# One hybrid layer (short convolution and RWKV-7): VectorE's order in phase 1 taken from a gap-filling clock, and general buffers handed out by the kernel

## The chip, the cores and the metric

The kernel runs on one core of one Trainium2 chip. The metric is device microseconds of one launch; 3 runs of the kernel before took 3189.91, 3191.65 and 3194.61 us, median 3191.65. The profile is one more execution of the same program.

## The reference

The input is 2048 rows of a new sequence and 8 x 4 rows of running ones, 1024 wide, all float32. What is computed, cut to its core:

```python
h = rmsnorm(x, norm_g)
p = h @ w_in                       # 4 x 1024 conv, 4 x 1024 + 128 rwkv, 2 x 1024 gate columns
u = cg * xin;  y_c = bg * conv3(u) * silu(zc)          # short convolution branch
xm = p_rwkv + (prev - p_rwkv) * mu_shift               # token shift, then r, k, v, wd, ad, zr
def step(S, inp):                                      # RWKV-7, 16 heads of 64, one step a token
    sa = einsum(S, -kk_t)
    S = S * d_t + sa * (kk_t * a_t) + v_t * k_t
    return S, einsum(S, r_t)
y_r = (groupnorm(ys) * ln_w + ln_b + bonus) * silu(zr)
m = sigmoid(gc) * (y_c @ w_out_c) + sigmoid(gr) * (y_r @ w_out_r)
y = rmsnorm(x + m @ w_o, final_g)
```

New convolution, shift and RWKV states are returned as well.

## The kernel before

**Tiling.** The sequence is cut into 4 sets of 512 tokens (NT); the last set carries the 32 running rows. Activations stand transposed, 128 channels by 512 tokens. Every float32 product is made of three fp32r matmuls of a high and a low part (XH, XL; whl holds both parts of a block of weights), so one block of 128 output channels is 8 x 3 matmuls of 512 columns into one bank `ip` (proj, L266). Weights are split into the two parts in the first set (ScalarE's cast, VectorE's subtraction, L225 and L249), stored, and loaded again ready split in later sets.

**Phase 1** (to about 2650 us) goes through the sets; in each through 8 pairs of heads, 32 pairs of set and heads in all. The main stream is the projection blocks (xin, cg, zc, bg and the two gates for the convolution, k, r, v, z for the next pair), whose results VectorE and ScalarE take out of the bank. Beside it run side tasks, Python generators (class Side, L309): keys (decays and scaled keys of the next pair), solve (a triangular inversion by 31 steps of two short VectorE operations, tt and X, behind a transpose Mi<-Mc, L930), merge, load, chain, out. The chain (rwkv_chain, L1091) is the recurrence: 8 steps a pair, each one TensorE `pa` = S x AR, VectorE `us` (two operations), TensorE `pb` = Xbd x us, the copy to `SV` (VectorE one half, then ScalarE the other, L1067), TensorE `pb` = BKt x SV, VectorE `S` (two operations). Near the end of phase 1 the first output products (oc) join the main stream. **Phase 3** is the rest of the output products and the final norm.

**What sets the order.** The program is traced by Python. A class Clock (L42) keeps a time for each engine and for each written box of a tile; every traced instruction is booked at the end of its engine's booked work or when its inputs are there, whichever is later (add, L91), with costs in ns from cost (L130). Side.run (L325) is called after each main matmul. It goes on with a side task only when the share of main work done asks for it, when the results it asked for are ready by the clock, and, for tasks that are not urgent, when VectorE's booked work reaches less than BACKLOG = 1800 ns past TensorE's. So the clock decides at which place among the main matmuls a side task's matmuls stand. After the trace the framework's compile-time scheduler puts the instructions of each engine in order, by trace order and by its own timing: one that it holds for not ready lets a later one go ahead. The order is then fixed; on the chip each engine takes its own list in turn and waits on semaphores.

The general buffers are the pool `tmp` (L403), eight buffers of 576 float32 a partition; the framework's scheduler gives out whichever is free.

Of the kernel before, what the change touches and what calls it, by code (L numbers as in the profile page):

```python
# [16 lines left out]
P = 128  # L17
# [23 lines left out]

class Clock:  # L42
# [3 lines left out]
    def __init__(self):  # L46
        self.t = dict.fromkeys(("PE", "DVE", "ACT", "POOL", "SP"), 0.0)
        self.log, self.home = {}, {}
        self.mode = (128, 128)
        self.held = {"DVE": [], "POOL": []}  # L50
# [25 lines left out]

    def name(self, ap):
        return self.home.get(ap.tensor.name, ap.tensor.name)
# [8 lines left out]

    def ready(self, aps):
        return max([e[4] for ap in aps for e in self._hits(ap)], default=0.0)

    def add(self, eng, outs, ins, cost, lag=60.0):  # L91
        start = max([self.t[eng]] + [e[4] for ap in ins for e in self._hits(ap) if e[6] != eng] +
                    [e[5] for ap in outs for e in self._hits(ap)])
        if eng == "POOL" or eng == "DVE" and sum(ap.space != PSUM for ap in ins) > 1:
            for s, e in self.held["POOL" if eng == "DVE" else "DVE"]:
                if s < start + cost and start < e:
                    start = e
            self.held[eng] = self.held[eng][-60:] + [(start, start + cost)]
        end = start + cost
        self.t[eng] = end  # L100
# [3 lines left out]
        for ap in outs:  # L104
            for p0, p1, f0, f1 in self.boxes(ap):
                old = self.log.setdefault(self.name(ap), [])
                old[:] = [e for e in old if not (p0 <= e[0] and e[1] <= p1 and f0 <= e[2] and e[3] <= f1)][-95:]
                old.append([p0, p1, f0, f1, end + lag, end, eng])


class Traced:
# [5 lines left out]
    def __getattr__(self, op):  # L117
        f = getattr(self.eng, op)

        def call(*a, **k):  # L120
# [5 lines left out]
            self.clock.add(self.name, outs, ins, self.cost(op, outs[0], ins, k), 200.0 if self.name == "PE" else 60.0)  # L126
# [3 lines left out]
    def cost(self, op, out, ins, k):  # L130
        n = out.free_size()
        if self.name == "PE":
            if op == "transpose":
                return 109.0
            lhs, rhs = k["lhsT"], k["rhs"]
            if rhs.dtype == F32R:
                mode, t = (P, P), 8 + 0.45 * n
            else:
                part = [next(x for x in (32, 64, 128) if v <= x) for v in (lhs.ap[0][1], lhs.free_size())]
                mode, t = tuple(part), 2 * max(0.84 * max(lhs.free_size(), n), 26.0) / (1 if part == [P, P] else 1.9)  # L140
            t += 170 * (mode != self.clock.mode)
            self.clock.mode = mode
            return t
        if self.name == "DVE":
            per = {"transpose": 1.6, "tensor_tensor_scan": 2.1}.get(op, 1.05)
            if op == "tensor_reduce":
                n = ins[0].free_size()
            return 150 + per * n
        if self.name == "ACT":
            return 200 + 0.84 * n + 90 * max(0, len(ins) - 1)  # L150
# [5 lines left out]
class Queue:  # L156
# [5 lines left out]
    def store(self, out, in_):  # L162

        self.due.append((out, in_))
        self.flush(2)

    def flush(self, most):
        while self.due and (len(self.due) > most or self.clock.ready([self.due[0][1]]) < self.clock.t["PE"]):
            self.dma_start(*self.due.pop(0))
# [10 lines left out]
def hybrid_kernel(tc, x_prompt, x_sample, state_conv, state_shift, state_rwkv, norm_g, w_in, conv_w,  # L180
# [26 lines left out]
    wraw_p = ctx.enter_context(tc.tile_pool(name="wraw", bufs=4))  # L207
    whl_p = ctx.enter_context(tc.tile_pool(name="whl", bufs=4))
    dram = ctx.enter_context(tc.tile_pool(name="dram", bufs=1, space=DRAM))
    ps_ip = ctx.enter_context(tc.tile_pool(name="ps_ip", bufs=3, space=PSUM))  # L210
# [98 lines left out]
    class Side:  # L309
# [15 lines left out]
        def run(self, upto, force=False):  # L325
# [3 lines left out]
            while self.given < goal and self.f0 <= upto and (force or max(self.due, pt_free(self.banks)) <= clock.t["PE"] and (  # L329
                    self.kind in URGENT or clock.t["DVE"] < clock.t["PE"] + BACKLOG)):  # L330
# [68 lines left out]
    nwt = ctx.enter_context(tc.tile_pool(name="nwt", bufs=1))  # L399
    con = ph1.enter_context(tc.tile_pool(name="con", bufs=1))  # L400
    xp = ph1.enter_context(tc.tile_pool(name="xp", bufs=1))
    rw = ph1.enter_context(tc.tile_pool(name="rw", bufs=1))
    tmp = ph1.enter_context(tc.tile_pool(name="tmp", bufs=8))  # L403
    ep = ph1.enter_context(tc.tile_pool(name="ep", bufs=2))
    sm = ph1.enter_context(tc.tile_pool(name="sm", bufs=2))
    ps_t = ph1.enter_context(tc.tile_pool(name="ps_t", bufs=2, space=PSUM))
    ps_a = ph1.enter_context(tc.tile_pool(name="ps_a", bufs=2, space=PSUM))
    ps_b = ph1.enter_context(tc.tile_pool(name="ps_b", bufs=1, space=PSUM))
# [22 lines left out]
    def stat_tile(i, xt, m):  # L431
        junk = tmp.tile([P, TW], F32, name="tmp").bitcast(BF16)[:, 0:D]
        A.activation(out=junk[0:m], in_=xt[0:m], func=AF.Square, accum_out=rstd[0:m, i:i + 1])

# [53 lines left out]
    V.transpose(X0.rearrange("p a b -> p (a b)"), xo0.rearrange("p a b c -> p (a b c)"))  # L488

# [61 lines left out]
    def to_cols(q, xt, cl, eng):  # L551
# [7 lines left out]
        split(XH[:, q * KG:(q + 1) * KG, cl:cl + P], XL[:, q * KG:(q + 1) * KG, cl:cl + P], xf, eng)  # L559

# [67 lines left out]
    def mixed_block(th, key, src, mb, alloc, end=None):  # L628
# [24 lines left out]
        def fin():  # L653
            if th < LAST:
                G.tensor_copy(carry[:, mb:mb + 1], o["q"][:, NT:NT + 1])
            if end:
# [18 lines left out]
    def conv_blocks(th, b):  # L675
# [25 lines left out]
        def cg_end():  # L701
            u = o["u"]
            cv = o["cv"] = ep.tile([P, NT + NSAMP], F32, name="cv", bufs=1)
# [24 lines left out]
        def zc_end():  # L728
            G.tensor_tensor(out=o["cv"][:, 0:nt], in0=o["cv"][:, 0:nt], in1=o["tz"][:, 0:nt], op=ALU.mult)

# [8 lines left out]
        def gate(nm, base, dst):  # L739
# [10 lines left out]
            def end():  # L750
                SP.dma_start(out=dst[th][b], in_=g["t"][:, 0:nt])
            return Block((nm, th, b), wcol(base, b), evac, begin, end)
# [22 lines left out]
    def rkvz_blocks(th, p):  # L775
# [14 lines left out]
        def z_end(zT):  # L790
# [3 lines left out]
            V.scalar_tensor_tensor(out=sz[:, 0:nt], in0=sz[:, 0:nt], scalar=1.0, in1=zT[:, 0:nt], op0=ALU.add, op1=ALU.mult)  # L794
            cur[(th, p)] = (got["r"], got["k"], got["v"], sz)
# [12 lines left out]
    def rwkv_keys(th, p, o):  # L808
# [20 lines left out]
        if samp:  # L829
# [3 lines left out]
            V.reciprocal(ss[0:NSAMP, 2 * TPS:], ss[0:NSAMP, 2 * TPS:])  # L833
        yield W["norm"], [up], 2
# [17 lines left out]
        if samp:  # L852
            V.tensor_tensor_scan(out=Gs[:, n:nt], data0=rst_s, data1=L[:, n:nt], initial=0.0, op0=ALU.mult, op1=ALU.add)
        yield W["scan"], [Gs[:, 0:nt]]
# [12 lines left out]
        A.activation(out=Pi[:, 0:nt], in_=Gs[:, 0:nt], func=AF.Exp, scale=DECAY)  # L867
# [755 lines left out]
```

## Time and profile before

| | |
|---|---|
| median of 3 runs | 3191.65 us |
| the profiled execution | 3193.32 us, span 3191.6 us |
| granted TensorE clock over the span | 0.992 |
| PE busy | 3092.0 us (97%), 21530 matmuls |
| PEld busy | 2596.5 us (81%) |
| DVE busy | 1992.5 us (62%), 5704 instructions |
| ACT busy | 1241.9 us (39%) |
| POOL busy | 309.6 us (10%) |
| chain that ended last | PE 69%, DVE 18%, ACT 5%, issue 5%, DMA 3% |

PE is TensorE's matmuls, PEld its weight loads, DVE is VectorE, ACT ScalarE, POOL GpSimd. All compute instructions come through one helper (L121) and all DMAs of SyncE through another (L172), so rows are told apart by tile names and not by lines: `ip` is a bank of a projection, `pt` a general PSUM bank, `pa`, `pb`, `us`, `SV` and `S` are the chain's. "x2" behind a float32 matmul is its two passes. A matmul's end is modelled, so matmuls that follow each other overlap in the rows.

### The profile page before, as it was taken

How to read it: one execution, taken by the hardware profiler on the slowest of the kernel's cores; microseconds unless marked ns; L12 is line 12 of the kernel's file. 1: busy time of each engine (PE TensorE's matmuls, PEld its weight loads, DVE VectorE, ACT ScalarE, POOL GpSimd, SP SyncE). 2: the span in 40 equal slices, each digit the busy share in tenths (PEclk: the TensorE clock that was granted, in tenths of full speed). 3: DMA queues.
4: the chain of work that ended last, by engine and by line, in shares of the span. 5: the costliest groups of instructions: out<-in, count | busy, mean ns of one | idle time of the engine just before them, and what ended most of it. 6: DMA issues, size and time to landing. Idle time of an engine off the chain costs nothing.

```text
span 3191.6 us, 55625 instructions
## 1 busy us (share of the span) xinstructions
PE 3092.0 (97%) x21530; PEld 2596.5 (81%) x21530; DVE 1992.5 (62%) x5704; ACT 1241.9 (39%) x2571; POOL 309.6 (10%) x517
## 2 busy tenths in 40 slices
PE   7999999999999999999999999999999999999998
PEld 6777777887777778877777789989889889778896
DVE  5687777776666666666666676766677664443332
ACT  5454445444333434434443334344444432211201
POOL 2011111111000001100101010000000000000000
PEclk9999999999999999999999999999999999999999
DMA  8786666644444444444444444434443469988863
GB/s 267 258 267 220 213 212 220 207 173 148 146 162 160 155 159 159 169 157 153 159 153 158 159 147 142 138 127 139 144 143 135 138 223 318 363 337 304 316 241 120
DMA packets 241504, 615.09 MB, mean 193 GB/s; under 512 B 33931, under 2 KB 143620, under 8 KB 187479
## 3 DMA queue, kind: packets, MB, share of 16 engines
q1 hardware_dynamic: 241094, 611.00, 55.8%
q8 instruction: 170, 2.79, 0.4%
q14 instruction: 96, 0.78, 0.1%
q0 software_dynamic: 144, 0.52, 0.0%
HBM read 452.10 MB, written 159.36 MB: 192 GB/s over the span
## 4 chain that ended last, share of the span: by engine, by line
PE 69%; DVE 18%; ACT 5%; issue 5%; DMA 3%; POOL 1%; SPq 0%; ACTq 0%; DVEq 0%; POOLq 0%
PE ip L121 49%; PE pt L121 10%; PE po L121 6%; PE pb L121 3%; DVE X L121 2%; DVE tmp L121 2%; DVE tt L121 2%; ACT tmp L121 2%; DVE Mi L121 2%; DVE whl L121 1%; DVE us L121 1%; PE pa L121 1%; DVE S L121 1%; DMA wraw<-in_w_in_dram 1%; ACT Xbd L121 1%
## 5 line engine op out<-in xcount | busy, mean ns | idle before, releaser
L121 PE MATMUL ip<-XH,whl 128*128 128x512 f32 (+3 forms) x7776 | 2105.1, 351 | 6.6 <-DVE gt L121 3.9
L121 PEld LDWEIGHTS ip<-XH,whl 128*128 128x128 f32 x7776 | 1342.0, 190 | 178.3 <-issue 27.5
L121 PE MATMUL ip<-XL,whl 128*128 128x512 f32 (+3 forms) x3888 | 1364.0, 351 | 2.7 <-POOL XL L121 2.6
L121 PEld LDWEIGHTS ip<-XL,whl 128*128 128x128 f32 x3888 | 738.5, 190 | 79.0 <-issue 7.0
L121 DVE TENSOR_TENSOR X<-X,tt 128x60 f32<-128x60 f32 (+24 forms) x992 | 211.7, 213 | 27.5
L121 DVE TENSOR_TENSOR tt<-Mi,X 128x60 f32<-128x60 f32 (+24 forms) x992 | 209.9, 212 | 27.4
L121 DVE SCALAR_TENSOR_TENSOR S<-pb,pe,sp 64x64 f32<-64x64 f32 x512 | 143.8, 281 | 106.6 <-PE pb L121 100.5
L121 ACT ACTIVATE sp<-S,pe 128x128 f32<-128x128 f32 x256 | 99.5, 400 | 244.7 <-DVE S L121 241.2
L121 ACT ACTIVATE tmp<-ip,vec 128x512 f32<-128x512 f32 (+2 forms) x174 | 103.2, 593 | 231.6 <-PE ip L121 230.2
L121 ACT COPY SV<-pb 64x64 f32<-64x64 f32 x256 | 53.3, 208 | 329.2 <-DVE SV L121 325.5
L121 DVE TENSOR_TENSOR whl<-wraw,whl 128x1024 fp32r<-128x1024 f32 x105 | 134.2, 1279 | 58.0 <-ACT whl L121 57.7
L121 PE MATMUL po<-whl,MH 128*128 128x512 f32 x544 | 170.4, 394 | 0.0
L121 DVE TENSOR_TENSOR us<-pa,P 64x64 f32<-64x64 f32 x512 | 110.2, 215 | 45.2 <-PE pa L121 33.7
L121 PEld LDWEIGHTS pb<-us,Xbd 128*128 128x128 f32 x512 | 85.9, 189 | 56.9 <-PE ip L121 21.5
L121 PE MATMUL ip<-RH,whl 128*128 128x512 f32 (+2 forms) x512 | 128.4, 341 | 1.7 <-DMA whl<-w_or 1.6
L121 PEld LDWEIGHTS pb<-SV,BKt 128*128 128x128 f32 x512 | 85.1, 189 | 54.6 <-ACT SV L121 45.9
L121 ACT CAST whl<-wraw 128x1024 fp32r<-128x1024 f32 x105 | 109.5, 1044 | 50.5 <-DMA wraw<-in_w_out_r_dram 14.8
L121 PE MATMUL pb<-SV,BKt 128*128 128x128 f32 x512 | 107.3, 291 | 17.4 <-ACT SV L121 17.3
L121 DVE TENSOR_TENSOR GM<-pt,mask_p 128x512 f32<-128x512 f32 x128 | 82.4, 685 | 64.4 <-PE pt L121 64.4
L121 PEld LDWEIGHTS po<-whl,MH 128*128 128x128 f32 x544 | 102.2, 188 | 24.0 <-DVE whl L121 0.3
L121 PE MATMUL pb<-us,Xbd 128*128 128x64 f32 x512 | 90.1, 258 | 23.7 <-DVE us L121 23.1
L121 ACT COPY Xbd<-Xo 32x256 f32<-32x256 f32 x128 | 88.1, 688 | 64.0 <-DVE Xo L121 61.9
(494 smaller groups left out, 3838.6 us busy)
## 6 DMA issues: line engine op xcount, KB each, us to landing
wraw<-in_w_in_dram SPq DMA_DIRECT2D x81, 512.0 KB
whl<-w_k SPq DMA_DIRECT2D x24, 1024.0 KB
whl<-w_r SPq DMA_DIRECT2D x24, 1024.0 KB
whl<-w_v SPq DMA_DIRECT2D x24, 1024.0 KB
whl<-w_z SPq DMA_DIRECT2D x24, 1024.0 KB
whl<-w_xin SPq DMA_DIRECT2D x24, 1024.0 KB
whl<-w_cg SPq DMA_DIRECT2D x24, 1024.0 KB
whl<-w_zc SPq DMA_DIRECT2D x24, 1024.0 KB
```

The source lines that it names most:

```text
L121: r = f(*a, **k)
```

## The change

Four things, all at trace time. (1) Clock.add books an operation of VectorE, ScalarE or GpSimd into the first gap among the last 200 booked ones that it fits in, from 3000 ns before TensorE's time on, never ahead of an operation of the same engine on the same tensor. TensorE's and SyncE's bookings are appended as before. (2) In phase 1 each VectorE instruction is noted with its begin time; behind phase 1 the list is sorted by it, and each instruction gets an edge to the one in front of it that orders the two and has no wait. (3) The costs are others, for TensorE by tiling and with a delay to the reader of its own. (4) The buffers `tmp` become eight buffers with fixed names; a class Ring gives out the one whose last use ends first by the clock, and the program frees each by a call. Tiles of other pools get names by which the clock knows which buffer they share. The instructions themselves, the loops, the weights of the side tasks and their spans are not changed.

```diff
     def add(self, eng, outs, ins, cost, lag=60.0):
-        start = max([self.t[eng]] + [e[4] for ap in ins for e in self._hits(ap) if e[6] != eng] +
+        start = max([self.t["PE"] - PAST if eng in self.busy else self.t[eng]] + [e[4] for ap in ins for e in self._hits(ap) if e[6] != eng] +
+                    [e[5] for ap in (*ins, *outs) for e in self._hits(ap) if e[6] == eng] +
+                    [self.touched.get((eng, ap.tensor.name), 0.0) for ap in (*ins, *outs)] +
                     [e[5] for ap in outs for e in self._hits(ap)])
+        if eng in self.busy:
+            start = self.gap(eng, start, cost)
...
+    def gap(self, eng, start, cost):
+        b = self.busy[eng]
+        if len(b) >= 200:
+            start = max(start, b[0][1])
+        i = len(b)
+        while i and b[i - 1][1] > start:
+            i -= 1
+        for s, e in b[i:]:
+            if s >= start + cost:
+                break
+            start = max(start, e)
+        return start
...
+class Ring:
...
+            home = min(self.open, key=self.ends)
+            self.open.remove(home)
+            t = self.pool.tile(self.shape, dtype, name="tmp", tag=home)
...
     def cost(self, op, out, ins, k):
...
-                mode, t = (P, P), 8 + 0.45 * n
+                mode, t, late = (P, P), 8 + 0.4375 * n, 175 + 0.43 * n
+            elif mode == (P, P):
+                t, late = max(1.667 * n + 3, 216.0), max(382.0 if n >= P else 328.0, 175 + 1.7 * n)
...
+            if mode != self.clock.mode:
+                t, late = t + 165, late + 225
+                self.clock.mode = mode
+            return t, late - t + SLACK
         if self.name == "DVE":
-            per = {"transpose": 1.6, "tensor_tensor_scan": 2.1}.get(op, 1.05)
+            per = {"transpose": 1.12 if n <= 256 else 1.86, "tensor_tensor_scan": 2.1, "reciprocal": 6.1}.get(op, 1.05)
...
-            return 150 + per * n
+            one = op == "scalar_tensor_tensor" and isinstance(k["scalar"], bass.AP)
+            return 145 + per * n + 58 * one
...
-                    self.kind in URGENT or clock.t["DVE"] < clock.t["PE"] + BACKLOG)):
+                    self.kind in URGENT or clock.load("DVE") < BACKLOG)):
...
-    tmp = ph1.enter_context(tc.tile_pool(name="tmp", bufs=8))
+    tmp = Ring(ph1.enter_context(tc.tile_pool(name="tmp", bufs=1)), [P, NT + 64], 8, clock)
...
     finish_sides()
+    clock.planning = False
+    for ops in clock.begun.values():
+        ops.sort(key=lambda o: o[0])
+        for (_, a), (_, b) in zip(ops, ops[1:]):
+            tc.add_manual_dep(b, a.name, mybir.DependencyInfo(
+                mybir.DependencyClass.NoSync, mybir.DependencyReason.DATA), reason="keep_in_program_order")
```

A matmul's result is ready for a reader on another engine 60 + (late - t + SLACK) ns after its booked end, with SLACK = 60; before it was 200 ns for each. A VectorE or GpSimd operation that reads two tiles of SBUF is kept off the intervals in which the other one of the two engines is booked with such an operation, in both kernels.

## Rows read from the trace of the kernel before

**Rows 1.** Stretches: us, busy us and count by engine, clock, DMA share, GB/s.

```profile
0.00:50.00 50.00, 30.10 (x195) 27.93 (x196) 28.44 (x67) 23.18 (x35) 18.51 (x55) 0.93 0.77 251
50.00:850.00 800.00, 771.09 (x5017) 611.10 (x5017) 569.79 (x1530) 386.42 (x727) 97.73 (x147) 0.99 0.65 213
850.00:1850.00 1000.00, 986.01 (x6536) 781.72 (x6533) 643.78 (x1944) 403.79 (x847) 102.51 (x189) 1.00 0.46 157
1850.00:2650.00 800.00, 782.06 (x6944) 724.78 (x6943) 546.12 (x1763) 329.58 (x781) 72.04 (x105) 0.99 0.45 151
2650.00:3192.00 542.00, 522.71 (x2847) 450.96 (x2845) 204.34 (x401) 98.96 (x182) 18.80 (x21) 0.99 0.78 284
```

**Rows 2.** TensorE's waits: who for whom, us in total, times, longest us.

```profile
PE pb L121 <- DVE us L121: 23.1, 39, 1.6
PE pb L121 <- ACT SV L121: 17.3, 29, 1.4
...
PE pt L121 <- DVE T L121: 3.5, 5, 1.0
PE pt L121 <- ACT Wm L121: 3.4, 7, 1.1
...
PE pa L121 <- DVE S L121: 1.9, 3, 0.9
```

**Rows 3.** Timeline from 258 us: start, us, engine, operation, [idle before <-releaser].

```profile
257.80 0.49 PE L121 MATMUL pa<-S,AR 128*128 128x128 f32 x2
...
258.35 2.05 DVE L121 STREAM_TRANSPOSE Mi<-Mc 128x1024 f32<-128x1024 f32 x1 [0.61 <-ACT Mc L121]
...
259.28 0.40 PE L121 MATMUL ip<-XL,whl 128*128 128x512 f32 x1
...
259.51 0.39 PE L121 MATMUL ip<-XH,whl 128*128 128x512 f32 x1
260.43 0.45 DVE L121 TENSOR_TENSOR us<-pa,P 64x64 f32<-64x64 f32 x2
...
261.02 0.41 PE L121 MATMUL pb<-us,Xbd 128*128 128x64 f32 x2 [1.12 <-DVE us L121]
```

**Rows 4.** Weight loads by form: count, busy us, mean ns, idle us before them, releasers.

```profile
L121 PEld LDWEIGHTS ip<-XH,whl 128*128 128x128 f32 x7776 | 1342.0, 190 | 178.3 <-issue 27.5 <-DVE gt L121 4.1 <-DVE whl L121 2.3
...
L121 PEld LDWEIGHTS pa<-S,AR 128*128 128x128 f32 x512 | 89.3, 190 | 24.8 <-DVE S L121 11.4
...
L121 PEld LDWEIGHTS pb<-us,Xbd 128*128 128x128 f32 x512 | 85.9, 189 | 56.9 <-PE ip L121 21.5 <-issue 17.8 <-DVE us L121 8.2
L121 PEld LDWEIGHTS pb<-SV,BKt 128*128 128x128 f32 x512 | 85.1, 189 | 54.6 <-ACT SV L121 45.9
```

**Rows 5.** Timeline from 941.5 us.

```profile
941.86 1.28 POOL L121 TENSOR_TENSOR cv<-cv,tmp 128x512 f32<-128x512 f32 x1 [12.73 <-DVE tmp L121]
...
942.17 1.52 DVE L121 TENSOR_TENSOR tmp<-tmp 128x512 fp32r<-128x512 f32 x1
...
943.62 0.21 DVE L121 COPY SV<-pb 64x64 f32<-64x64 f32 x1
...
944.12 0.38 PE L121 MATMUL pb<-SV,BKt 128*128 128x128 f32 x1 [0.67 <-ACT SV L121]
```

**Rows 6.** Timeline from 957.5 us; six tt and X operations up to `us`.

```profile
957.87 0.21 DVE L121 TENSOR_TENSOR tt<-Mi,X 128x54 f32<-128x54 f32 x1
957.88 0.38 PE L121 MATMUL pa<-S,AR 128*128 128x128 f32 x2
...
959.36 0.45 DVE L121 TENSOR_TENSOR us<-pa,P 64x64 f32<-64x64 f32 x2
...
959.95 0.41 PE L121 MATMUL pb<-us,Xbd 128*128 128x64 f32 x2 [0.29 <-DVE us L121]
```

**Rows 7.** Waits of all engines: who for whom, us in total, times, longest us.

```profile
ACT SV L121 <- DVE SV L121: 327.1, 169, 4.9
...
DVE tmp L121 <- ACT tmp L121: 146.3, 70, 5.3
```

More of the change, by code (lines that the diff above doesn't have):

```diff
@@ L49, in __init__ @@
         self.mode = (128, 128)
+        self.busy = {"DVE": [], "ACT": [], "POOL": []}
+        self.touched = {}
+        self.begun, self.planning = {}, False
         self.held = {"DVE": [], "POOL": []}
@@ L86, in _hits, with load @@
                         yield e
+    def gap(self, eng, start, cost):
[10 more added lines that the diff above has]
+        return start
+    def load(self, eng):
+        return sum(e - max(s, self.t["PE"]) for s, e in self.busy[eng][-60:] if e > self.t["PE"])
     def ready(self, aps):
@@ L125, in call @@
             ins += aps if "out" in k else aps[1:]
[L126 removed]
+            c = self.cost(op, outs[0], ins, k)
+            c, late = c if isinstance(c, tuple) else (c, 0.0)
+            at = self.clock.add(self.name, outs, ins, c, late + 60.0)
+            if self.clock.planning and self.name in PLANNED:
+                self.clock.begun.setdefault(self.name, []).append((at, r.ins))
             return r
@@ L160, in __init__, with store @@
         self.eng, self.clock, self.due = eng, clock, []
-    def store(self, out, in_):
-        self.due.append((out, in_))
+    def store(self, out, in_, then=None):
+        self.due.append((out, in_, then))
         self.flush(2)
@@ L168, in flush @@
         while self.due and (len(self.due) > most or self.clock.ready([self.due[0][1]]) < self.clock.t["PE"]):
-            self.dma_start(*self.due.pop(0))
+            out, in_, then = self.due.pop(0)
+            self.dma_start(out, in_)
+            if then:
+                then()
     def dma_start(self, out, in_):
@@ L488, in hybrid_kernel @@
     V.transpose(X0.rearrange("p a b -> p (a b)"), xo0.rearrange("p a b c -> p (a b c)"))
+    tmp.free(xo0)
     rst = con.tile([P, NT], F32, name="rst")
@@ L559, in to_cols @@
         split(XH[:, q * KG:(q + 1) * KG, cl:cl + P], XL[:, q * KG:(q + 1) * KG, cl:cl + P], xf, eng)
+        tmp.free(xf)
     def prep(th, half):
@@ L655, in fin @@
                 G.tensor_copy(carry[:, mb:mb + 1], o["q"][:, NT:NT + 1])
+            tmp.free(o["q"])
             if end:
@@ L702, in cg_end @@
             u = o["u"]
+            tmp.free(o["xs"])
             cv = o["cv"] = ep.tile([P, NT + NSAMP], F32, name="cv", bufs=1)
@@ L833, in rwkv_keys @@
             V.reciprocal(ss[0:NSAMP, 2 * TPS:], ss[0:NSAMP, 2 * TPS:])
+        tmp.free(sq)
         yield W["norm"], [up], 2
@@ L867, in rwkv_keys @@
         A.activation(out=Pi[:, 0:nt], in_=Gs[:, 0:nt], func=AF.Exp, scale=DECAY)
+        tmp.free(Gs)
         yield W["exp"], [Pi[:, 0:nt], Pt]
@@ L881, in rwkv_keys @@
         V.tensor_tensor(out=ta[:, 0:n], in0=pt, in1=ta[:, 0:n], op=ALU.mult)
+        tmp.free(sb)
         if samp:
@@ L889, in rwkv_keys @@
             V.tensor_tensor(out=ta[:, n:nt], in0=pt[:, 0:NSAMP], in1=ta[:, n:nt], op=ALU.mult)
+            tmp.free(sb)
         yield W["key"]
@@ L907, in rwkv_keys @@
             yield W["key"]
+        tmp.free(ta, Pi, Pt)
         V.scalar_tensor_tensor(out=kh[:, 0:nt], in0=rT[:, 0:nt], scalar=rkh[:, p:p + 1], in1=kh[:, 0:nt],
@@ L923, in rwkv_keys @@
             V.tensor_tensor(out=bv[:, c0:c1], in0=pt[:, 0:c1 - c0], in1=vT[:, c0:c1], op=ALU.mult)
+        tmp.free(bh, bl)
         yield W["bones"]
@@ L1215, in rwkv_out @@
         V.tensor_reduce(out=mu_, in_=y2, axis=AX.X, op=ALU.add)
+        tmp.free(y2)
         yield from rsq_steps(mu_, [P, k], 1.0 / 64, GN_EPS)
@@ L1239, in rwkv_out @@
         SP.dma_start(out=yr_d[th][p // 2][:, p % 2, :], in_=yo[:, 0:nt])
+        tmp.free(yo)
     def whole(bl):
@@ L1264, in end @@
         def end():
-            SP.store(gc_d[th][b], o["g"][:, 0:NT])
+            SP.store(gc_d[th][b], o["g"][:, 0:NT], lambda g=o["g"]: tmp.free(g))
         return Block(("oc", th, b), w_out_c[0][:, b * P:(b + 1) * P], evac, begin, end)
@@ L1363, in hybrid_kernel @@
     put_vec(NB, nrow)
+    tmp.free(vrow)
     def derived(nm, src, n, s1, s2, base=0):
```

113 lines of the change are left out of this document (89 added, 24 removed).

## Prediction

> **What bounds the kernel now.** I read the stretches first [rows 1]: TensorE is busy 771, 986 and 782 of 800, 1000 and 800 us in the three stretches of phase 1, and VectorE 570, 644 and 546. So TensorE sets the time, and a gain can only come out of its idle time: 28.9 + 14.0 + 17.9 = 60.8 us in phase 1, beside 19.9 us in the first 50 us and 19.3 us behind phase 1. VectorE itself is at most 71% busy; faster or fuller work on it is worth nothing by itself.
>
> Next, who ended TensorE's waits [rows 2]. Five rows belong to phase 1 and to results that VectorE makes or hands on: `us` 23.1 us in 39 waits, `SV` 17.3 in 29 (ScalarE's copy, which follows VectorE's), T 3.5, Wm 3.4, S 1.9: 49.2 us in 83 waits. Nearly all of it is the RWKV chain: TensorE `pa`, VectorE `us`, TensorE `pb`, VectorE and ScalarE `SV`, TensorE `pb`, VectorE `S`. A wait hides a little more than it shows: a 512 column matmul is drawn 0.39 to 0.40 us long, though the next one starts 0.23 us after it, by the two `ip` rows of [rows 3], so each wait costs about 0.16 us beyond its idle time: 83 x 0.16 = 13. That makes 62 us. The other end is given by the weight loads [rows 4]: those of the chain stood idle 24.8 + 56.9 + 54.6 = 136.3 us in 1536 loads; an ordinary load stands idle 178.3 / 7776 = 0.023 us, 35 us for as many, so up to 101 us could be the chain's, short waits included.
>
> Then what VectorE did in such a wait, in three places. (a) [rows 3] The chain's `pa` is done at 258.3, but VectorE starts the transpose Mi<-Mc at 258.35; it takes 2.05 us, `us` begins at 260.43, and TensorE stands 1.12 us. (b) [rows 5] A subtraction tmp<-tmp with two SBUF inputs begins at 942.17 beside a GpSimd operation (941.86 to 943.14) and takes 1.52 us; the copy to SV comes behind it, and TensorE stands 0.67 us. (c) [rows 6] `pa` is done at 958.26, yet `us` comes at 959.36, behind the short tt and X operations of another pair's inversion, and TensorE stands 0.29 us. In all three a VectorE operation that nobody on TensorE waited for went ahead of one that it did.
>
> **The change part by part.**
>
> 1. *Order of VectorE.* Nothing is added or taken from the instructions: VectorE's come in the order of the clock's begin times, tied by edges that order and don't wait, so the price of the edges is nothing. What the clock now does: an operation takes the first gap that it fits in, and it can't push what is booked already. In (a) either `us` was booked first, and the 2 us transpose goes behind it, or the transpose was, and then the clock books `us` behind it and the chain's next step is issued when that is due, with projection matmuls in between. The clock's transposes of 1024 elements go from 150 + 1.6 x 1024 = 1788 ns to 145 + 1.86 x 1024 = 2050, against 2.05 us in the row: an error of 0.26 us goes. In (b) the clock keeps the subtraction out of the GpSimd interval and lets the copy to SV go first; the 0.67 to 0.83 us go. In (c) the tt and X operations are booked at 145 + 1.05 x 54 = 202 ns each (207 before), while six of them took 959.36 - 957.87 = 1.49, or 248 ns each; a run of six is booked 0.28 us too short, which is the whole wait of 0.29. So (c) stays. Ends of this term: nothing of the 62 us goes, or all. Kinds (a) and (b) carry the long waits, (c) and its like the short ones, and I know neither share; I take half: -31 us.
>
> 2. *The clock's TensorE.* The clock is what decides how many projection matmuls go between two chain steps. A 512 column matmul is booked at 8 + 0.4375 x 512 = 232 ns instead of 238, against 0.23 us [rows 3]: over a 2 us hop the old clock issued 3%, or 0.05 us, too little. The delay from the end of `pa` to a reader goes from 200 to 296 ns (175 + 1.7 x 128 - 216 + 60 + 60), so nearly 0.1 us more cover for each hop. That works on the short waits, the 101 - 62 = 39 us: between 0 and -39. The 256 steps of the chain make 768 hops; I take one in eight to be short by 0.05 us: -5.
>
> 3. *The general buffers.* The eight buffers stay eight, and each user now gets the one whose last use ends first by the clock. It adds no instruction. Before, any free one would do at compile time; now a wrong guess of the clock makes a writer wait for one given buffer, behind a store on the DMA queue at worst. No row of TensorE's waits names such a buffer with more than 1 us; bounds 0 and +5, I take 0.
>
> 4. *New misfits.* The clock now also fills gaps on ScalarE and GpSimd, whose order isn't kept by edges, and it books VectorE closely where it used to append. Where a booking is wrong, VectorE waits with everything behind it. Bounds: 0, and the slower rival below; I take +8, one new 0.5 us wait in every second of the 32 pairs.
>
> 5. *Not touched.* The matmuls, the weight splits' number, the DMAs, the first 50 us and what lies behind phase 1 (39 us of idle time) stay. The extra calls of `free` issue nothing.
>
> Sum: -31 - 5 + 0 + 8 = -28 us. The profiled execution took 3193.3 us with a span of 3191.6, and its 1.7 us around the span don't change: 3193.3 - 28 = 3165.3. The median of the runs shown, 3191.65, lies 1.7 us below that execution, so the forecast is 3164 us, 0.9% faster.
>
> A rule of the Trainium skill speaks against this. First the row: the tt and X operations are 0.21 us long and start 0.248 us apart [rows 6]. The page "VectorE: DVE Perf Modes", section "The DRAIN you can't avoid", says that after each operation the next doesn't start until the pipeline is empty. By that, no run of short operations can be booked back to back at 202 ns, and a plan that packs them is late wherever a run stands ahead of the chain; this would make the first rival out of the forecast, and the trace agrees with the rule.
>
> **The rivals.**
>
> *The waits only move (no change).* The bookings of short operations are 46 ns short, 62 of them in each of 32 pairs, 2.9 us a pair, and the waits come from this and not from which operation goes first; or the old order was nearly the clock's already, so that the change does little of what it says. Then what (a) and (b) give back, (c) takes again. For it: 207 ns has become 202, the wrong way. Against it: (a) and (b), where the long operation is one that the clock prices well. Price: half of the 31 us gained, with 11 us lost to packing (one late `us` of 0.34 us in each of 32 pairs) and the 8 us: -15 + 11 + 8, within 6 us of no change, 3188 to 3196.
>
> *The fixed order stalls (slower).* VectorE's place in the chain now hangs on the clock's view of ScalarE. ScalarE stands 327 us behind SV, 169 times, and VectorE 146 us behind ScalarE's tmp, 70 times, 2.1 us each [rows 7]; the clock fills such holes on ScalarE with later work, and the chip may not. Where it is wrong, an operation that waits 2.1 us stands in front of `us`, `SV` or `S`, and the chain's next matmul waits on TensorE. Against it: TensorE's filler covers a part, and before, too, the order was fixed ahead of the run. It decides from 31 + 5 = 36 us / 2.1 = 17 such stalls on, of 768 hops; at one in each of the 32 pairs, 67 us, it costs 67 - 36 = +31: 3223 us.
>
> *More goes than I think.* All 62 us and part of the short waits: 3191.65 - 62 + 8 - 10 = 3128. For it: the three places are of one kind, a clock that was not the one that ordered VectorE. Against it: (c).
>
> **How the numbers follow.** Forecast, 3145 to 3183: 0.52. More: 0.14. No change: 0.15. Slower: 0.19. What a measurement of this kernel can tell from no change is 0.2%, 6.4 us, 3185.3 to 3198.0. So faster 0.52 + 0.14 = 0.66, same 0.15, slower 0.19. The range that should hold 8 in 10 reaches from 3125 (all the waits gone) to 3212 (the slower rival at about 27 stalls); the forecast's own is 3145 to 3183.
>
> **What would show it.** In the changed profile the rows `pb` <- `us` and `pb` <- `SV` should have halved in total and in their longest; no Mi<-Mc should stand between a finished `pa` and its `us`; the subtraction beside a GpSimd operation should come after the copy to SV or last 0.7 us; weight loads of `pb` should stand idle for less than 40 us in each row. TensorE's idle time in phase 1 should be 35 us and in the first 50 us and behind phase 1 as before. Wrong if those two rows are as large as before with other operations ahead of `us`; the slower rival if VectorE's waits for ScalarE's tmp have grown and TensorE's waits with them. Wrong in its premise if the span moves while TensorE's idle time doesn't, say by more switches of the array's tiling.

## The result and the profile after

The change made the kernel slower: 3204.23 us, median of 7 runs (3202.79 to 3205.48), against 3191.65 us for the kernel before in the same job. The ratio is 1.0042, 95% interval 1.0030 to 1.0053. The forecast was 3164. The profiled execution has a span of 3201.2 us, 9.6 us more than before; two traces are compared by these spans.

The stretches of the changed kernel (us, busy us and count of TensorE, its weight loads, VectorE, ScalarE, GpSimd; clock, DMA share, GB/s), to be laid beside [rows 1]:

```profile
0.00:50.00 50.00, 29.95 (x193) 28.16 (x194) 26.79 (x64) 24.04 (x36) 19.09 (x55) 1.00 0.76 235
50.00:850.00 800.00, 773.61 (x5042) 613.66 (x5040) 566.48 (x1533) 393.12 (x733) 92.29 (x147) 0.99 0.66 214
850.00:1850.00 1000.00, 987.88 (x6578) 786.83 (x6577) 640.65 (x1950) 407.91 (x848) 112.53 (x190) 1.00 0.46 158
1850.00:2650.00 800.00, 774.70 (x6829) 712.22 (x6828) 560.28 (x1764) 330.89 (x780) 70.88 (x106) 0.99 0.44 146
2650.00:3201.20 551.20, 528.92 (x2897) 457.40 (x2895) 205.94 (x396) 95.96 (x175) 17.86 (x20) 0.99 0.78 285
```

TensorE's idle time in phase 1 is 26.4 + 12.1 + 25.3 = 63.8 us, where the prediction had 35 and before had 60.8. Less idle time in the first two stages, 7.4 us more in the third. Behind 2650 us it is 22.3 instead of 19.3, and the busy time is 3.1 us more in all.

Who ended TensorE's waits (us in total, times, longest us), beside [rows 2]:

```profile
PE pb L218 <- ACT SV L218: 16.6, 42, 2.1
PE ip L218 <- DVE whl L218: 14.0, 6, 6.1
PE ip L218 <- DVE GM L218: 10.7, 1, 10.7
PE ip L218 <- DVE tmp L218: 8.4, 8, 3.0
PE pb L218 <- DVE us L218: 6.9, 21, 0.4
PE ip L218 <- DVE wraw L218: 4.0, 1, 4.0
...
PE pt L218 <- ACT tmp L218: 3.4, 5, 1.2
PE ip L218 <- DVE tt L218: 2.8, 2, 2.1
...
PE ip L218 <- DVE XL L218: 2.0, 1, 2.0
...
PE pt L218 <- DVE T L218: 1.7, 3, 0.9
...
PE pa L218 <- DVE S L218: 1.4, 2, 1.1
...
PE pt L218 <- ACT Wm L218: 0.6, 2, 0.3
```

These rows are of the whole span; the one wait of 10.7 us behind GM lies in the first 50 us, where before had one of 10.2. The five rows of the chain (`us`, `SV`, T, S, Wm) went from 49.2 us in 83 waits to 27.2 in 70: 22.0 us less. In the window of phase 1, 50 to 2650 us, the idle time that the view gives to a releaser was 58.0 us in all and is 61.5, so all other rows rose from 58.0 - 49.2 = 8.8 to 61.5 - 27.2 = 34.3 us. They are few and long, and their matmuls are mostly `ip`, the projections: the filler that was to cover the chain now waits itself.

**Where it happened.** The projections and output products are the same matmuls in the same number in every version, so I took the start of the 400th, 800th and so on from each trace and subtracted that of before. The table has what was lost (+) or won (-) in each stretch, named by its time in the kernel before; the sum is taken at the last of these matmuls. Two traces of all but the same schedule (after and e12, or e17 and e18 up to 2649) differ by up to 2.5 us in a stretch, so less than that means nothing. Sets change at 627 to 724, at about 1260 (where nothing is lost) and at 1815 to 1905, the third change, and phase 1 hands over at 2649 to 2702; the column "rest" is what remains of the total.

| kernel | 0-113 | 113-246 | 246-627 | 627-724 | 724-1815 | 1815-1905 | 1905-2649 | 2649-2702 | rest | sum |
|---|---|---|---|---|---|---|---|---|---|---|
| after | +9.0 | 0.0 | -12.7 | +6.4 | -11.1 | +9.5 | +5.6 | +6.0 | -3.0 | +9.8 |
| e12 (SLACK 61) | +9.3 | +0.8 | -11.7 | +6.4 | -11.4 | +9.8 | +6.9 | +4.6 | -3.1 | +11.6 |
| e14 (145.3) | +8.2 | +0.3 | -4.1 | +8.8 | -10.9 | +9.2 | +5.6 | +5.4 | -4.3 | +18.2 |
| e15 (144.7) | +7.7 | -0.1 | -12.0 | +8.5 | -9.5 | +12.1 | +6.1 | +4.3 | -0.3 | +16.7 |
| e2 (tt, X dearer) | +6.5 | -3.1 | -11.1 | +11.0 | -15.6 | +10.3 | +0.2 | +13.7 | -1.0 | +10.9 |
| e4 (prep free) | +10.2 | +2.0 | -9.0 | +6.6 | -8.9 | +1.6 | +6.0 | +13.7 | -3.8 | +18.4 |
| e9 (free in four) | -1.2 | +8.7 | -8.9 | +9.8 | -11.0 | -3.1 | +8.2 | +4.7 | -1.9 | +5.1 |
| e16 (free at third) | +11.3 | +0.7 | -11.5 | +6.3 | -11.0 | -3.1 | +10.5 | +4.2 | -1.3 | +6.0 |
| e17 (free first, third) | -0.3 | +9.2 | -11.0 | +6.4 | -10.7 | -3.1 | +7.9 | +4.7 | -1.4 | +1.7 |
| e18 (free first, third, end) | -0.9 | +10.2 | -13.5 | +6.4 | -10.7 | -3.1 | +7.6 | +5.6 | -2.1 | -0.5 |
| e1 (no edges) | -3.8 | +8.6 | +5.4 | +9.8 | +5.4 | -2.4 | +10.7 | +2.1 | -0.9 | +34.9 |
| e6 (no ring) | +12.5 | +1.2 | -5.6 | +6.2 | -8.1 | +11.7 | +6.5 | +14.0 | -1.3 | +37.2 |
| e7 (old costs) | +7.5 | +4.1 | -7.0 | +5.3 | +19.1 | +10.4 | +13.4 | +11.3 | -2.7 | +61.4 |
| e8 (before, edges) | +1.2 | +2.4 | -6.6 | +3.7 | +6.0 | +2.8 | +10.0 | +4.2 | -3.7 | +20.0 |
| e5 (ring alone) | -2.6 | +0.4 | +3.5 | +2.9 | +3.3 | -0.3 | +3.2 | +2.4 | -2.1 | +10.7 |
| e10 (before, 151) | -0.7 | +0.4 | -1.1 | -2.9 | +5.3 | -1.2 | +11.5 | +2.8 | -2.5 | +11.6 |
| e11 (before, 149) | +0.6 | +2.1 | +0.5 | +0.5 | +3.6 | -1.2 | +9.6 | 0.0 | -0.6 | +15.0 |

In the steady stretches (246 to 627, 724 to 1815) the changed kernel wins 23.8 us, in the kind of place that the forecast had in mind (e1, without the edges, loses 10.8 there). It loses 30.9 in four short ones, and 5.6 in the last set. Of the four, the 6.4 us at 627 to 724 are not lost for good: between 724 and 857 the changed kernel wins 6.9, and e1 does so too (7.1), so this is work that moved across the boundary.

**The places of the prediction.** VectorE and GpSimd at (a) and (b) in the changed kernel (start us, us, engine, operation, [idle before <-releaser]), beside [rows 3] and [rows 5]:

```profile
260.28 0.45 DVE L218 TENSOR_TENSOR us<-pa,P 64x64 f32<-64x64 f32 x2 [1.28 <-PE pa L218]
260.76 2.08 DVE L218 STREAM_TRANSPOSE Mi<-Mc 128x1024 f32<-128x1024 f32 x1
...
938.09 1.28 POOL L218 TENSOR_TENSOR cv<-cv,tmp 128x512 f32<-128x512 f32 x1 [1.24 <-DVE tmp L218]
938.55 0.22 DVE L218 COPY SV<-pb 64x64 f32<-64x64 f32 x1 [0.54 <-PE pb L218]
938.69 1.23 DVE L218 TENSOR_TENSOR tmp<-tmp 128x512 fp32r<-128x512 f32 x1
```

Both are turned round: `us` goes ahead of the transpose and the copy to SV ahead of the subtraction, and the places cost TensorE nothing. Weight loads (busy us, mean ns, idle us before them), beside [rows 4]:

```profile
L218 PEld LDWEIGHTS pa<-S,AR 128*128 128x128 f32 x512 | 88.6, 188 | 20.2 <-DVE S L218 7.4
L218 PEld LDWEIGHTS pb<-us,Xbd 128*128 128x128 f32 x512 | 86.5, 188 | 35.4 <-PE ip L218 17.0 <-issue 6.4 <-DVE us L218 0.3
L218 PEld LDWEIGHTS pb<-SV,BKt 128*128 128x128 f32 x512 | 81.3, 188 | 64.2 <-ACT SV L218 58.7 <-issue 0.8
```

`us` is cured, `SV` isn't. Its longest wait shows why; ScalarE, VectorE and TensorE in the changed kernel:

```profile
363.98 0.18 DVE L218 COPY SV<-pb 64x64 f32<-64x64 f32 x1
364.09 2.69 ACT L218 COPY Xbd<-Xo 32x256 f32<-32x256 f32 x4 [0.52 <-DVE Xo L218]
366.81 0.21 ACT L218 COPY SV<-pb 64x64 f32<-64x64 f32 x1
367.07 0.49 PE L218 MATMUL pb<-SV,BKt 128*128 128x128 f32 x2 [2.09 <-ACT SV L218]
```

VectorE's half of SV is done at 364.16, but ScalarE has four copies for another pair ahead of its own half, 2.69 us, and ScalarE's order isn't held.

**The long stops.** At the third change VectorE waits, then everything behind it is late (VectorE and TensorE of the changed kernel):

```profile
1865.06 0.75 DVE L218 TENSOR_SCALAR wraw<-wraw,rstd 128x1024 f32<-128x1024 f32 x1
1870.37 1.22 DVE L218 TENSOR_TENSOR wraw<-wraw 32x1024 f32<-32x1024 f32 x1 [4.56 <-DMA wraw<-in_norm_g_dram]
...
1889.83 0.86 PE L218 MATMUL ip<-XH,whl 128*128 128x296 f32 x2 [1.94 <-DVE tmp L218]
...
1894.90 0.58 PE L218 MATMUL ip<-XL,whl 128*128 128x296 f32 x1 [1.98 <-DVE XL L218]
```

The operation needs a transfer of 128 KB. The chain of work that ended last shows what this transfer itself stood behind (start us, us, what):

```profile
1864.59 0.67 PE ip L218 x4
1865.27 4.97 DMA wraw<-in_norm_g_dram
```

The kernel's clock had the operation follow the one before it by 1.22 us (1846.88 after 1845.66 in its own time); on the chip it follows by 5.31, which is 4.09 too late. No other VectorE step of this stretch is misjudged by half as much. The short tt and X operations slip 0.05 us each against the clock, as the prediction had it.

The clock misjudged two things. It let the transfer begin at 1839.69, 6.0 us ahead of the operation at 1845.66, but on the chip it was issued 0.2 us behind that operation's start, when four matmuls of TensorE had read what stood in its buffer before. In the program these matmuls are issued behind the transfer, so the clock didn't know of them. And it booked 2.45 us for the transfer (2000 ns and 131072 / 290), where the chain has 4.97. The first is the larger: issued 6 us earlier, a transfer of 4.97 us would have been in time, while one of 2.45 us issued at 1865.27 would still have come at 1867.72 for an operation due at 1866.28.

By the Trainium skill, page "DMA: Bandwidth & Descriptors", section "Anatomy of one DMA — SWDGE (gpsimd) path", a transfer on GpSimd's path takes some 2.0 us and its bytes by 436e3 a us; worked out for 128 KB that is an estimate of 2.3 us, near the clock's 2.45. This transfer is issued by SyncE, not on that path, and the measured 4.97 decides. The DMA engines were 65% busy in this stretch; whether that made it long, no run shows.

The windows of before, of the changed kernel and of e16 show what followed:

```profile
1875.00:1895.00 20.00, 17.88 (x124) 17.27 (x123) 16.75 (x49) 6.79 (x16) 2.78 (x4) 0.83 0.50 158
```

```profile
1855.00:1875.00 20.00, 17.83 (x167) 16.69 (x166) 13.13 (x29) 5.99 (x14) 2.43 (x2) 1.00 0.65 208
1875.00:1895.00 20.00, 12.72 (x87) 10.43 (x87) 18.69 (x59) 7.46 (x16) 4.22 (x5) 0.84 0.21 49
1895.00:1905.00 10.00, 9.97 (x86) 9.64 (x87) 6.98 (x26) 4.76 (x10) 0.00 (x0) 0.81 0.30 107
```

```profile
1875.00:1895.00 20.00, 18.28 (x159) 16.79 (x160) 19.05 (x65) 7.75 (x16) 3.26 (x5) 1.00 0.41 117
```

In the 20 us from 1875 on VectorE is full (18.69) and TensorE idle for 7.3 us. That VectorE is full is not enough: in e16, which has no edges here, it is as full (19.05) and TensorE idle for 1.7. What differs is what VectorE does first. A part of the 12.6 us between the changed kernel and e16 (+9.5 and -3.1 in the table) is TensorE's granted clock, which changed between its two levels, 1.2 and 2.4 GHz, in these windows. In and behind the stops above its mean is 0.84 and 0.81, so (1 - 0.84) x 20 + (1 - 0.81) x 10 = 5.1 us of full clock are missing; before has 0.83 in one window, 3.4 us, and e16 has 1.00. This is an estimate from the windows. By it, e16's win over before at this change is about what before itself loses by its clock.

When phase 1 ends VectorE stands behind a load of `gc` (changed kernel, then the kernel before and e18):

```profile
2679.03 0.42 DVE L218 SCALAR_TENSOR_TENSOR tmp<-tmp,ip 128x256 f32<-128x256 f32 x1 [10.01 <-DMA tmp<-gc]
2679.60 0.48 PE L218 MATMUL ip<-XH,whl 128*128 128x256 f32 x2 [2.98 <-DVE tmp L218]
```

```profile
2667.68 0.42 DVE L121 SCALAR_TENSOR_TENSOR tmp<-tmp,ip 128x256 f32<-128x256 f32 x1 [5.83 <-DMA tmp<-gc]
```

```profile
2668.62 0.42 DVE L219 SCALAR_TENSOR_TENSOR tmp<-tmp,ip 128x256 f32<-128x256 f32 x1 [10.58 <-DMA tmp<-gc]
```

Here the held order is not the cause. VectorE waits for this load in the kernel before as well, and in e18, whose order is free from 2610 us on, as long as in the changed kernel; e9 and e18 lose 4.7 and 5.6 us in this stretch, the changed kernel 6.0.

The first stretch is of another kind (changed kernel):

```profile
110.70 1.05 ACT L218 CAST whl<-wraw 128x1024 fp32r<-128x1024 f32 x1 [1.40 <-DMA wraw<-in_w_in_dram]
116.05 1.22 DVE L218 TENSOR_TENSOR whl<-wraw,whl 128x1024 fp32r<-128x1024 f32 x1
117.33 0.80 PE L218 MATMUL ip<-XH,whl 128*128 128x512 f32 x1 [6.11 <-DVE whl L218]
125.65 0.17 DVE L218 TENSOR_SCALAR nw<-rstd 128x13 f32<-128x13 f32 x1 [5.29 <-ACT tmp L218]
130.06 1.07 PE L218 MATMUL ip<-ident,wraw 40*128 40x40 f32 x8 [4.01 <-DVE wraw L218]
```

ScalarE's part of the weight split is ready at 111.75, VectorE's comes at 116.05 behind a run of tt and X operations; TensorE stands 6.11 us. Here the chip keeps the clock's times (the split is 0.4 us early against the operation before it): the plan itself has the split that late.

### The profile page after: what moved, and what is told of

Read it like the earlier page. It is cut to its first block, busy times and chain, and to the rows that moved or that the text cites. A ratio compares the mean times of both kernels' runs of the same rounds, so it can differ in the third digit from the quotient of the medians.

```text
span 3201.2 us, 55474 instructions
## 1 busy us (share of the span) xinstructions
PE 3095.1 (97%) x21530; PEld 2598.3 (81%) x21530; DVE 2000.1 (62%) x5704; ACT 1251.9 (39%) x2571; POOL 312.7 (10%) x517
## 4 chain that ended last, share of the span: by engine, by line
PE 71%; DVE 16%; ACT 4%; issue 4%; DMA 4%; POOL 1%; SPq 0%; ACTq 0%; DVEq 0%; POOLq 0%
PE ip L218 51%; PE pt L218 10%; PE po L218 6%; DVE tt L218 3%; DVE X L218 3%; PE pb L218 3%; ACT tmp L218 2%; DVE Mi L218 2%; DVE tmp L218 2%; PE pa L218 1%; DVE us L218 1%; DVE S L218 1%; DMA wraw<-in_w_in_dram 1%; DVE whl L218 1%; ACT Xbd L218 1%
## 5 line engine op out<-in xcount | busy, mean ns | idle before, releaser
L218 PEld LDWEIGHTS ip<-XH,whl 128*128 128x128 f32 x7776 | 1341.3, 190 | 204.1 <-issue 39.4
L218 PEld LDWEIGHTS po<-whl,MH 128*128 128x128 f32 x544 | 102.2, 188 | 23.8
L218 DVE SCALAR_TENSOR_TENSOR gt<-gt,ip 128x288 f32<-128x288 f32 (+2 forms) x67 | 36.5, 544 | 116.7 <-PE ip L218 102.7
L218 PE MATMUL po<-whl,ML 128*128 128x512 f32 x272 | 107.1, 394 | 0.0
```

The costliest lines, as they stand in the source:

```text
L218: r = f(*a, **k)
```

## The experiments

Theory A: holding the order loses. Rival B: short operations booked too short. Rival C: what loses is not the order but when the clock issues work, or the buffers. All are edits of the changed kernel unless said otherwise.

**e1.** `PLANNED = ('DVE',)` -> `PLANNED = ()`

> The changed kernel without the edges between VectorE's instructions; clock, costs and buffers stay changed. Theory A (the fixed order makes VectorE stand for inputs that come later than booked, DMA-fed ones above all, with the main stream's evacuations behind it): the long TensorE stops at 110 to 131 us (10.5 us), at 1885 to 1894 (7 us) and at 2668 to 2679 (5 us) go, some of the chain's waits on us come back (6.9 us towards 23): 3180 to 3192 us. Rival C (the new issue points and the buffers cost the time, not the order): stays at 3200 to 3208 us with the same stops.

3230.24 us, ratio to before 1.0121 (1.0107 to 1.0135). This is above the ranges of A and of C. A falls as a whole: the edges give 26 us, more than the neighbours below move. Without them the waits of the chain are back:

```profile
PE pb L218 <- DVE us L218: 34.2, 37, 2.3
PE pt L218 <- DVE T L218: 16.3, 9, 4.6
```

**e2.** `return 145 + per * n` -> `return (175 if short tt or X else 145) + per * n`

> The changed kernel with the inversion's short VectorE operations (tt and X) booked 30 ns dearer: 232 ns for 54 elements, where the trace shows 248 from start to start. Theory B (runs of short operations are booked too short, so that at the changes of set, where inversion, preparation and evacuations meet, VectorE is late): the stops at 650 to 663 and 1885 to 1894 us go or halve, 3192 to 3197 us, while those at 110 to 131 and 2668 stay. Theory A and rival C: 3202 to 3206 us, stops unchanged.

The edit takes in every `tensor_tensor` of less than 80 elements whose first input is not in PSUM. 3204.81 us, 1.0041 (1.0029 to 1.0054): nothing gained in the sum. By the table the losses at 627 to 724 and 1815 to 1905 are 11.0 and 10.3 us, not less than the 6.4 and 9.5 of the changed kernel, so B falls as far as this one schedule can tell.

**e3.** `c.add("SP", [out], [in_], size / 290.0, 2000.0)` -> `... 8000.0)`

> The changed kernel with a clock in which each DMA's data is there 8000 ns behind its booked end instead of 2000; the trace showed loads of 7.9 to 10.4 us at the places of the stops. Theory A: the stops at 110 to 131 and at 2668 us go, about -12 us: 3190 to 3194 us; the one at 1885 stays. Theory B and rival C: 3202 to 3206 us.

3283.02 us, 1.0286 (1.0271 to 1.0300), far outside every range. The clock's idea of a transfer also sets when all work is issued, so this run changed far more than the one wait, and it doesn't show what the late transfer costs.

**e4.** No edges for VectorE's operations of the side tasks that load and prepare weights and inputs:

```diff
+                    clock.loose = self.kind in ("first", "late", "prep")
...
-            if self.clock.planning and self.name in PLANNED:
+            if self.clock.planning and self.name in PLANNED and not self.clock.loose:
```

> The changed kernel in which VectorE's instructions of the first, late and prep side tasks (statistics and preparation of the next rows, loads for the first output products) get no edges and are placed by the compile-time scheduler; all others keep the clock's order. Theory A: 3186 to 3193 us, stops at 125 and 1885 us gone, the chain's gain (us 6.9 us) kept. Theory B: 3196 to 3201 us, the preparation being only a part of the crowd. Rival C: 3200 to 3208 us.

3208.96 us, 1.0048 (1.0034 to 1.0062), above all three ranges. The loss at the third change shrank from 9.5 to 1.6 us (the operation that waited there belongs to prep, so it is among those set free), that at the end of phase 1 grew from 6.0 to 13.7.

**e5 to e8** take the change apart. e5: before with `tmp = Ring(...)` and the calls of `free`. e6: `tmp = Ring(...)` -> a pool of 8. e7: the old `cost` and delays. e8: before with the edges, in the order of issue.

> The kernel before with one part of the change: the general buffers are handed out by the kernel (eight, the one whose last use ends first by the clock); clock, costs and order as before. Without the edges the changed kernel was 38 us slower than before, so something besides the order loses. If the buffers are it: 3215 to 3230. If the clock's new bookings are it (when TensorE's pieces are issued): within 6 us of 3191.7.

> The changed kernel with the general buffers given out as before (eight in a pool, any free one at compile time), all else as changed. If the buffers cost: 3170 to 3185. If they cost nothing: 3200 to 3208. If they are needed for the fixed order (a store or a reader behind a wrong buffer): slower, 3215 or more.

> The changed kernel with the old table of costs and the old delay of TensorE's results (200 ns), gap filling, order and buffers as changed. If the new costs issue TensorE's pieces at worse moments: 3175 to 3195. If the gap filling does so: 3200 to 3210. If the new costs are a help, without which the gap filling misplaces more: 3215 or more.

> The kernel before with edges alone: VectorE's instructions of phase 1 are held in the order in which the program issues them, clock, costs and buffers as before. If any fixed order of VectorE takes away the chain's waits as the edges did in the changed kernel (26 us): 3160 to 3175. If what the edges gain there is only the order that fits the gap-filling bookings, and before already had the order that fits its own: within 6 us of 3191.7. If the order of issue makes VectorE wait for late inputs: 3200 or more.

| | us | ratio to before |
|---|---|---|
| e5 ring alone | 3203.84 | 1.0040 (1.0028 to 1.0053) |
| e6 changed, no ring | 3230.81 | 1.0121 (1.0104 to 1.0137) |
| e7 changed, old costs | 3258.32 | 1.0211 (1.0197 to 1.0225) |
| e8 before, edges | 3217.79 | 1.0084 (1.0069 to 1.0099) |

e5 and e8, with one part alone, are slower than before; e1, e6 and e7, with one part taken out, are slower than the changed kernel. The gap filling was neither tried alone nor taken out. e6, e7 and e8 came out as the last of their three alternatives, e5 between its two. The parts don't add up: e5 loses 12 us with the ring alone, yet within the change the ring is worth 26.6. The 12 us are no more than a neighbour of before loses by one nanosecond (e10 and e11), so they don't price the ring; the others (26 to 54 us) are beyond that.

**e10 to e15** ask what a change without meaning does. e10 and e11: before with `return 151 + per * n` and 149 for 150. e13: before with BACKLOG 1810 for 1800. e12: SLACK 61 for 60. e14, e15: 145.3 and 144.7 for 145.

> The kernel before with one number of its clock moved by 1 ns: VectorE's fixed cost is 151 instead of 150. It means nothing, but the pieces are issued elsewhere from the 524th row of TensorE on. Theory, the time of before is a good draw among many equal schedules: 3196 to 3220, as for the part edits. Rival, the time follows the schedule smoothly: 3189 to 3194.

> As the one with 151, with 149: by the theory of the good draw 3196 to 3220, by the smooth one 3189 to 3194.

> The kernel before with BACKLOG 1810 ns instead of 1800, which means as little as the 1 ns; TensorE's rows part at the 1807th. If before is a good draw: 3196 to 3212, as its two other neighbours (3206.5, 3208.4). If those two were bad luck: 3189 to 3195.

> The changed kernel with one number of its clock moved by 1 ns: the delay on TensorE's results (SLACK) is 61 instead of 60. If each schedule is a draw: 3185 to 3230, some 5 us or more from 3204.2 on either side. If smooth: 3201 to 3207.

> The changed kernel with VectorE's fixed cost at 145.3 ns instead of 145; TensorE's rows part at the 475th, so that this is another draw, which the one with SLACK 61 was not (its stretches were those of the changed kernel within 2 us). If the changed kernel is an ordinary draw of its kind: 3195 to 3215 on either side of 3204. If it is a bad one: 3170 to 3195, and the order is worth its 28 us against the neighbours of before (3207). If a good one: 3210 to 3230.

> As the one with 145.3, with 144.7: ordinary draw 3195 to 3215, bad draw 3170 to 3195, good draw 3210 to 3230.

| neighbours of before | us | ratio | neighbours of after | us | ratio |
|---|---|---|---|---|---|
| e10 | 3206.47 | 1.0042 (1.0028 to 1.0056) | e12 | 3205.78 | 1.0044 (1.0029 to 1.0058) |
| e11 | 3208.42 | 1.0053 (1.0037 to 1.0069) | e14 | 3212.74 | 1.0074 (1.0060 to 1.0088) |
| e13 | 3192.59 | 1.0008 (0.9998 to 1.0017) | e15 | 3211.61 | 1.0070 (1.0054 to 1.0087) |

One nanosecond in the clock costs before 14 to 16 us, as much as the whole change; e13 costs it nothing. How far each is another schedule can be read from the order of TensorE's 21530 matmuls in the traces: e12 differs from the changed kernel in 6 places, so it is no draw of its own; e13 differs from before in 1322, e11 in 3538, e10 in 6585. By its expectation e13 speaks for bad luck of the other two. So that before is a good draw is likely and not shown: two of three neighbours lose, above all in the last set, where e10 and e11 lose 11.5 and 9.6 us between 1905 and 2649 and most versions in the table 5 us or more. e14 and e15 lie in the ranges of an ordinary and of a good draw at once. The pattern of the changed kernel is no accident: both win and lose in the same stretches as it does. With the kernels themselves the four of before have a mean of 3199.8 us and the four of after 3208.6. Whether the kinds differ by that can't be settled with four of each that spread over 17 and 9 us.

**e9, e16 to e18** take the edges out in stretches of the clock's time only:

```diff
+LOOSE = ((102e3, 136e3), (640e3, 700e3), (1833e3, 1884e3), (2610e3, 1e9))
         ops.sort(key=lambda o: o[0])
+        ops = [o for o in ops if not any(x <= o[0] < y for x, y in LOOSE)]
```

e16 has the third alone, e17 (102e3, 250e3) and the third, e18 those and the last.

> The changed kernel without the edges in four stretches of the clock's time alone (102 to 136, 640 to 700, 1833 to 1884 and from 2610 us on: where the sets change and phase 1 ends); everywhere else VectorE's order is held. In these the changed kernel loses 9.0 + 6.4 + 9.5 + 6.0 = 31 us against the kernel before, in the stretches between it gains 21. The kernel without any edges lost 1.2 + 3.7 + 2.8 + 4.2 = 12 there, with the plain pool in between. Theory, the held order stands behind a late DMA or statistic there: 3204 - 19 = 3185, 3178 to 3192. Rival, the work that is issued there and not its order loses: 3200 to 3210.

> The changed kernel without edges in the clock's 1833 to 1884 us alone (the change from the third set to the fourth). There the one that was free in four stretches gained 12.6 us on the changed kernel (-3.1 instead of +9.5 against before), while it lost as much in and behind others. If the stretches add up: 3204.2 - 12.6 = 3191.6, 3188 to 3195. If the loss only moves on: 3198 to 3206.

> The changed kernel without edges from 102 to 250 and from 1833 to 1884 us of the clock. Free at the third change it lost 12.0 us against the kernel before up to 246 us; free from 102 to 136, 7.4 (the loss came behind the stretch); with no edge at all, 3.6. If the long freedom keeps the latter: 3194.5 - 12.0 + 3.6 = 3186, 3182 to 3190, which is less than either kernel by a little. If the statistics' lateness comes back behind the stretch as before: 3190 to 3198.

> As the one before, and free from 2610 us on as well, where the kernel free in four stretches lost 4.7 instead of 6.0. If it adds up: 1 us less than the one before, 3181 to 3190. If the end of phase 1 needs the held order for the samples' work: 3190 or more.

e9 took 3197.53 us, ratio 1.0020 (1.0011 to 1.0029); e16 3194.45, 1.0015 (1.0006 to 1.0024); e17 3195.50, 1.0013 (1.0004 to 1.0022); e18 3195.35, 1.0017 (1.0008 to 1.0026). e9 and e17 came out above what they were forecast, and one reason stands in the expectations: the figures given there for the kernel without any edges (1.2 + 3.7 + 2.8 + 4.2, and 3.6 up to 246 us) are those of e8, before with edges; e1 has -3.8, +9.8, -2.4 and +2.1, and 4.8 up to 246. e18 shows that freedom at the end changes nothing.

e16 came out as "the stretches add up". With the order free at the third change alone, the loss of 9.5 us there became a win of 3.1, as in e9, e17 and e18, and no VectorE wait for that transfer is left. The kernel is 4.6 us above before in the same job, where the changed one was 12.6 above: 8.0 us gained. So at this change it is the held order that costs. That it costs because of the late transfer is read from the trace, and e4, which frees the waiting operation with the rest of prep, agrees with 1.6; no run moved the transfer alone.

At the first stretch e17 was wrong by 9 us: the loss moves behind 113 us, to other waits of the same statistics and inversions. TensorE in e17:

```profile
109.05 0.50 PE L219 MATMUL ip<-XH,whl 128*128 128x512 f32 x1 [1.22 <-DVE whl L219]
...
119.09 0.31 PE L219 MATMUL pt<-T,GM 32*32 32x32 f32 x2 [3.76 <-DVE T L219]
...
129.57 1.07 PE L219 MATMUL ip<-ident,wraw 40*128 40x40 f32 x8 [6.39 <-DVE wraw L219]
```

At 627 to 724 freedom was no help (+9.8 in e9 instead of +6.4), and what is lost there comes back behind it. At the start freeing the order gains little: up to 246 us e9, e17 and e18 lose 7.5, 8.9 and 9.3 us, the changed kernel 9.0. That VectorE is given too much at once there is a reading and not shown. The table narrows it down: in the same stretch e1, e6 and e7 lose 4.8, 13.7 and 11.6 us, e5 and e8 -2.2 and 3.6, and of the four parts only the gap filling is in all that lose and in none of the others. That points at it and is no proof. No version beat the kernel before.

## Why the prediction was wrong

- *Step 1, order of VectorE, -31.* Right in its mechanism, and nearly in size: the chain's idle time fell by 22.0 us in 13 fewer waits, by the prediction's 0.16 us each another 2: -24. Places (a) and (b) were turned round, (c) stayed: in the middle stage `us` had 3.3 us before and 4.4 after, while `SV` fell from 9.6 to 4.1. What I left out is that ScalarE's half of the copy to SV comes when ScalarE's own order, which isn't held, gets to it. In the first stage `SV` rose from 4.5 to 8.0 us, and its longest wait there is ScalarE's queue. e1 shows that the edges did it: without them `us` has 34.2 us.
- *Step 2, clock's costs, -5.* The chain's weight loads stood idle for 119.8 us instead of 136.3, but the long waits alone fell by more. By the prediction's own measure the short waits were 101 - 62 = 39 us; now, with ordinary loads idle for 204.1 / 7776 = 0.026 us (40 us for 1536), they are 119.8 - 40 - 27.2 - 70 x 0.16 = 41. The 5 us are not seen. As a term by itself it was badly posed: e7 shows the new costs worth 54 us within this clock.
- *Step 3, buffers, 0.* No wait for such a buffer appeared, as forecast (the transfer at the third change waited for a buffer, but one of another pool, wraw). But they move the issue points: e5 lost 12 us and e6, without the ring, 26.6. The bounds 0 and +5 had no room for that, though e5 alone is within what a neighbour loses.
- *Step 4, new misfits, +8.* This step failed. It is +25.5 us in phase 1 (34.3 - 8.8), and not one 0.5 us wait in every second pair but 19 stops of 0.5 us or more, up to 6.1 us, where before had 5, and 14 of them at the start or where sets change. I priced them from the steady chain, since all my rows came from there, and read no row at the changes. What the runs showed in its place: at the third change, the held order behind one operation whose transfer comes later than booked (9.5 us lost, a win of 3.1 without the edges). At the start and at the end of phase 1 freeing the order gained nothing, and the cause stays open.
- *Step 5, not touched.* The first 50 us held (20.05 for 19.9). Behind phase 1 it is 3.0 us more: the load of `gc` above.

Sum as measured: -22.0 + 25.5 + 0.2 + 3.0, and 3.1 of busy time, are +9.8 against a span that grew by 9.6.

Of the rivals, "the fixed order stalls" was right in kind at the third change: it had an operation that waits standing in front of those that TensorE needs. It was wrong in place. VectorE's waits for ScalarE's tmp fell (below, beside [rows 7]); the wait that counts is for a transfer:

```profile
ACT SV L218 <- DVE SV L218: 292.8, 171, 4.5
...
DVE tmp L218 <- ACT tmp L218: 101.9, 34, 5.3
```

"The waits only move" holds for phase 1 as a whole (-22.0 and +25.5), not by its mechanism: e2 booked the short operations 30 ns nearer to the trace and gained nothing. And a rival was missing: that before is a good draw. Its two neighbours by one nanosecond are 14 to 16 us slower (a third neighbour, e13, is not), so even the right mechanism may have had to win that first. A part of the 12.6 us by which the change lost can be this draw; how much stays open.

## What to carry to other kernels

Before pricing a change to a planner, time two or three neighbours of the kernel as it stands: if a meaningless nanosecond costs 0.5%, the kernel may be a lucky draw, and a change must win more than that to be seen. Price a held order at the places where the plan's guesses are worst (transfers whose buffer comes free later than the plan knows, changes of stage), not in the steady loop; a plan that is right to 0.05 us an operation there was wrong by 4 us here. And where two engines hand on one result, holding the order of one of them leaves the other's queue as the wait; holding ScalarE's order as well was not tried.

## What the runs showed of the hardware

The transfer of 128 KB took 4.97 us of the chain of waits in a stretch in which the DMA engines were 65% busy, twice the 2.45 us that the kernel's clock has for it. In a run of tt and X operations each starts 0.05 us later than the clock books it; e2 is the only run that changed this booking, and the time stayed the same (3204.81 for 3204.23 us).
